# Rows of tokens from the vector engine's 32x32 transposes and a detour through DRAM, in place of TensorE's transposes

## The chip, the cores and the metric

The kernel runs on one core of one Trainium2 chip. The metric is the device time of one execution in microseconds (us). Three runs of the kernel before took 2768.79, 2769.45 and 2770.16 us; the median, 2769.45, is the time before.

## The reference

One step of a one-layer hybrid encoder for 256 prompt tokens and 64 sample tokens (320 together, the T of the code), model width 4096. What matters here is the outer frame; the mixer itself (attention heads and state-space heads behind the projection `w_in`) is untouched.

```python
def trunk_layer(x, p, ...):                       # x: (1, 256, 4096) or (1, 64, 4096)
    h = rmsnorm(x, norm_pre)
    m, k_new, v_new, conv_new, ssd_new = hybrid_mixer(h, ..., w_in, ..., w_out)
    x = x + rmsnorm(m, norm_post)
    e = p @ w_ple_proj                            # p has 256 features
    gate = jax.nn.sigmoid(x @ w_ple_gate)
    x = x + rmsnorm(gate * e, ple_norm)
    return x, ...                                 # y_prompt, y_sample: rows of tokens
```

`rmsnorm` divides a token's row by the root of its mean square and multiplies each feature by a weight. With r_m and r_g for the two factors of a token, the output is y = x + r_m * (m * norm_post) + r_g * (gate * e * ple_norm).

## The kernel before

**Weights.** All projections run with features on the partitions and the 320 tokens on the free axis. The weights come in blocks of 512 x 256 (512 KB, one DMA `raw` on SyncE's queue, line 155, four buffers). ScalarE rounds a block to `whi` (line 158), VectorE takes the rest `wlo` (line 159), three buffers each, and TensorE does 24 matmuls of 128 x 128 on 320 columns with the block (lines 163 to 165: whi*ahi, whi*alo, wlo*ahi). There are 720 blocks: 448 of `w_in`, 128 of `w_out`, then 128 of `w_ple_gate` and 16 half blocks of `w_ple_proj`. Eight blocks (kg 0 to 7) give one pair: two feature tiles of 128 rows, as two accumulators in PSUM. There are 16 pairs.

**Order.** `project` runs through the blocks; work behind a pair is a generator, and `tick` takes every pending generator one step further with each block. A scheduler turns the program into one fixed list of instructions for each engine, and each engine does its list in order, so an instruction that waits holds everything behind it on its engine. SyncE issues the DMAs in the order of its list too.

**From the output projection on.** `put_m` keeps the pairs of m, with `norm_post`, in eight group tiles. After r_m, `load_x2` forms x = xt + r_m * m for a group at a time, split into `ahi` and `alo`, while the first three gate pairs are projected together (`joint`, 8 x 3 blocks). This is the transition between the two phases. `put_pair` makes gate * e for a pair (`gate_out`, lines 335 to 346) and `two` with `ple_norm`. Between the gate pairs the half blocks of `w_ple_proj` make the next e (`embed`).

**Back to rows of tokens.** `to_token_rows` transposes each pair on TensorE (line 847; lines 854 and 855 for the sample's rows, once in two pairs) and ScalarE copies it out. `residual` does the same for x by products of `ahi` and `alo` with an identity (line 876; lines 882 and 884 for the sample): four units ahead of the end of the last gate pair, the other 16 behind it. After r_g, `finish` adds r_g * g to each unit on VectorE (line 920). SyncE stores eight column groups of 512: y_prompt by line 923, y_sample by line 926, whose pattern is `[2, 64, 256]`: two column halves, 64 tokens, 256 columns.

Of the kernel before, what the change touches and what calls it, by code (L numbers as in the profile page):

```python
# [41 lines left out]
def hymba_step(  # L42
# [17 lines left out]
    # what lives in one half of the kernel: the mixers, or the projections behind them  # L60
# [91 lines left out]
    def weights(src, kg, c0, nk=KG):  # L152
        """nk row tiles of NCOL columns, split exactly into two parts of 12 bits."""
# [13 lines left out]
    # Work behind a projection, as generators that pause between their stages; projections take  # L167
    # them one step further with each group of rows, so that the tensor engine finds their operands ready.
# [44 lines left out]
    def rsqrt_mean(out, total, n, shape):  # L213
        """out = (total / n + EPS) ** -0.5, with one step of Newton's method."""
# [8 lines left out]
    def factor_of(sqs, n):  # L223
        """The norm's factor of each token, on all partitions, from partial sums of squares."""
# [13 lines left out]
    class Squares:  # L238
        """Sum over `count` feature tiles of squares; the last one stays apart."""
# [3 lines left out]
        def add(self, make):  # L243
            """make(tile, soon) squares the next feature tile."""
# [16 lines left out]
    xt_dram = dram.tile([P, NK, T], F32, name="xt_dram")  # L261
    u_dram = dram.tile([P, 16, T], F32, name="u_dram")
    ssq = const1.tile([P, 3, NG], F32, name="ssq")
# [61 lines left out]
    def gate_in(g):  # L325
        """-g, bounded below as the exponential's argument is above."""
# [4 lines left out]
    def gate_out(es, vals, outs):  # L331
        """out = val / (1 + exp(-g)) for each e of gate_in(g); the quotient by one step of Newton's method."""
# [22 lines left out]
    def put_u(i, ap_mul):  # L355
        """Unit i (16 of each mixer) of the mixed output before its norm."""
# [10 lines left out]
    def to_rows(t, h, dst_p, dst_s, n):  # L367
        """A head's keys or values, back in rows of tokens."""
# [50 lines left out]
    def stick(h, i, q, k, vn, ck, cv, gss):  # L419
# [15 lines left out]
        # softplus(z), and log sigmoid(z) over z  # L435
# [33 lines left out]
    def steps():  # L469
        """dt of each token and head (tokens on partitions), dt * a, and decays."""  # L470
# [512 lines left out]
```

## Time and profile before

| what | us |
|---|---|
| median of three runs | 2769.45 |
| the profiled execution, its span (the only time of its own that its page gives) | 2768.3 |
| TensorE busy in it | 2741.7 (99%) |
| VectorE, ScalarE busy | 1450.8 (52%), 1110.9 (40%) |
| from the last gate matmul (2722.3) to the end | 46.0 |

The page's shares are of the span. "PEclk" in a row of windows is the granted clock of TensorE as a share of its full speed, 1.00 or 0.50 being its two levels, 2.4 and 1.2 GHz, and what lies between a mixture. In rows of instructions the arrow means "made from"; `L163` is line 163. The ends of matmuls are modelled; their distance in the chain of waits is the better price.

### The profile page before, as it was taken

How to read it: one execution, taken by the hardware profiler on the slowest of the kernel's cores; microseconds unless marked ns; L12 is line 12 of the kernel's file. 1: busy time of each engine (PE TensorE's matmuls, PEld its weight loads, DVE VectorE, ACT ScalarE, POOL GpSimd, SP SyncE). 2: the span in 40 equal slices, each digit the busy share in tenths (PEclk: the TensorE clock that was granted, in tenths of full speed). 3: DMA queues.
4: the chain of work that ended last, by engine and by line, in shares of the span. 5: the costliest groups of instructions: out<-in, count | busy, mean ns of one | idle time of the engine just before them, and what ended most of it. 6: DMA issues, size and time to landing. Idle time of an engine off the chain costs nothing.

```text
span 2768.3 us, 45230 instructions
## 1 busy us (share of the span) xinstructions
PE 2741.7 (99%) x18710; PEld 2713.2 (98%) x18710; DVE 1450.8 (52%) x2155; ACT 1110.9 (40%) x1551; POOL 241.5 (9%) x327
## 2 busy tenths in 40 slices
PE   9999999999999999999999999999999999999998
PEld 8999999999999999999999999999999989999997
DVE  4566666666666534435354453653333386454453
ACT  5443334433344333424333343543333354444441
POOL 0000010010000000000000000000101032121110
PEclk9999999999999999999999999999999999999997
DMA  7645454454454554555555455555444464444442
GB/s 236 194 120 145 132 149 138 127 164 127 143 148 134 149 153 143 151 149 146 152 143 157 140 150 161 168 162 159 148 150 152 137 191 147 150 144 151 149 142 84
DMA packets 419183, 414.13 MB, mean 150 GB/s; under 512 B 21792, under 2 KB 410784, under 8 KB 418976
## 3 DMA queue, kind: packets, MB, share of 16 engines
q1 hardware_dynamic: 418976, 411.24, 50.2%
q8 instruction: 146, 2.39, 0.3%
q14 instruction: 61, 0.50, 0.0%
HBM read 390.64 MB, written 20.55 MB: 149 GB/s over the span
## 4 chain that ended last, share of the span: by engine, by line
PE 96%; issue 1%; POOL 1%; DMA 1%; DVE 0%; ACT 0%; SPq 0%; DVEq 0%; POOLq 0%; ACTq 0%
PE acc L163 30%; PE acc L165 29%; PE acc L164 29%; POOL ug L817 1%; PE px L876 1%; DMA raw<-in_w_in_dram 1%; PE aux L665 1%; PE aux L372 0%; PE aux L492 0%; PE aux L557 0%; PE aux L847 0%; PE aux L453 0%; PE aux L666 0%; PE aux L426 0%; PE aux L651 0%
## 5 line engine op out<-in xcount | busy, mean ns | idle before, releaser
L163 PE MATMUL acc<-ahi,whi 128*128 128x320 f32 x5632 | 1757.6, 312 | 0.0
L165 PE MATMUL acc<-ahi,wlo 128*128 128x320 f32 x5632 | 1741.6, 309 | 3.6 <-DVE wlo L159 3.6
L164 PE MATMUL acc<-alo,whi 128*128 128x320 f32 x5632 | 1742.2, 309 | 1.3 <-DVE alo L819 1.2
L159 DVE TENSOR_TENSOR wlo<-raw,whi 128x1024 fp32r<-128x1024 f32 (+1 forms) x720 | 888.9, 1236 | 1119.6 <-ACT whi L158 1109.6
L158 ACT CAST whi<-raw 128x1024 fp32r<-128x1024 f32 (+1 forms) x720 | 747.1, 1038 | 1369.3 <-PE acc L164 1328.0
L165 PEld LDWEIGHTS acc<-ahi,wlo 128*128 128x128 f32 x5632 | 1058.5, 188 | 5.4 <-DVE wlo L159 5.4
L164 PEld LDWEIGHTS acc<-alo,whi 128*128 128x128 f32 x5632 | 1059.7, 188 | 2.5 <-DVE alo L819 2.3
L163 PEld LDWEIGHTS acc<-ahi,whi 128*128 128x128 f32 x5632 | 1059.3, 188 | 2.5
L252 POOL TENSOR_TENSOR stat<-stat,w 128x320 f32<-128x320 f32 x88 | 117.5, 1335 | 596.8 <-ACT w L779 404.6
L236 POOL TENSOR_TENSOR w<-ug 128x320 f32<-128x320 f32 x26 | 31.1, 1197 | 947.2 <-DVE ug L457 687.5
L335 ACT ACTIVATE w<-w 128x320 f32<-128x320 f32 (+1 forms) x96 | 45.1, 470 | 101.6 <-DVE w L328 101.5
L342 DVE SCALAR_TENSOR_TENSOR w<-w 128x320 f32<-128x320 f32 (+1 forms) x96 | 51.3, 541 | 16.3 <-ACT w L340 16.3
L236 POOL TENSOR_TENSOR w<-w 128x320 f32<-128x320 f32 x29 | 31.1, 1071 | 296.4 <-DVE w L346 296.4
L550 DVE SCALAR_TENSOR_TENSOR w<-w,vec 128x323 f32<-128x323 f32 x96 | 53.1, 553 | 2.1
L338 ACT ACTIVATE w<-w,tiny 128x320 f32<-128x320 f32 (+1 forms) x96 | 52.3, 560 | 2.9
L340 ACT ACTIVATE w<-w,shift 128x320 f32<-128x320 f32 (+1 forms) x96 | 52.2, 559 | 1.4
L344 DVE SCALAR_TENSOR_TENSOR w<-w 128x320 f32<-128x320 f32 (+1 forms) x96 | 49.6, 529 | 1.2
L545 POOL COPY ctail<-w 128x3 f32<-128x3 f32 x32 | 6.1, 190 | 328.3 <-DVE w L543 328.3
L328 DVE TENSOR_SCALAR w<-acc 128x320 f32<-128x320 f32 x32 | 15.6, 488 | 24.8 <-PE acc L165 24.7
L817 POOL TENSOR_TENSOR ug<-ug,two 128x320 f32<-128x320 f32 x16 | 23.7, 1486 | 43.2 <-DVE ug L816 43.2
L818 ACT CAST ahi<-ug 128x320 fp32r<-128x320 f32 x32 | 14.4, 461 | 25.8 <-POOL ug L817 22.4
L636 DVE TENSOR_SCALAR b<-le,dtah 128x256 fp32r<-128x256 f32 (+2 forms) x96 | 24.7, 292 | 0.0
(270 smaller groups left out, 1476.7 us busy)
## 6 DMA issues: line engine op xcount, KB each, us to landing
raw<-in_w_in_dram SPq DMA_DIRECT2D x448, 512.0 KB, 3.7
raw<-in_w_out_dram SPq DMA_DIRECT2D x128, 512.0 KB, 3.6
raw<-in_w_ple_gate_dram SPq DMA_DIRECT2D x128, 512.0 KB, 3.6
xt_dram<-ug SPq DMA_DIRECT2D x8, 640.0 KB, 6.2
two<-xt_dram SPq DMA_DIRECT2D x16, 320.0 KB, 3.3
b<-in_x_prompt_dram SPq DMA_DIRECT2D x16, 256.0 KB, 4.7
out_dram<-nat SPq DMA_DIRECT2D x32, 128.0 KB, 1.8
raw<-in_w_ple_proj_dram SPq DMA_DIRECT2D x16, 256.0 KB, 2.7
```

Source lines behind the costliest of these rows:

```text
L158: S.copy(hi, raw)
L159: V.tensor_sub(lo, raw, hi.bitcast(F32))
L163: PE.matmul(out, whi, xhi, start=start, stop=False)
L164: PE.matmul(out, whi, xlo, start=False, stop=False)
L165: PE.matmul(out, wlo, xhi, start=False, stop=stop)
L236: G.tensor_mul(sq, t, t)
L252: G.tensor_add(self.sum, self.sum, sq)
L338: S.activation(r, e, AF.Ln, scale=2.0 ** -62, bias=tiny)
L340: S.activation(r, r, AF.Exp, scale=-1.0, bias=shift)
L342: V.scalar_tensor_tensor(out=e, in0=e, scalar=1.0, in1=r, op0=ALU.add, op1=ALU.mult)
L550: V.scalar_tensor_tensor(out=c, in0=ext[:, j:j + XE], scalar=vec3[:, j * 32 + ct:j * 32 + ct + 1], in1=c, op0=ALU.mult, op1=ALU.add)
L817: (G if j % 2 else V).tensor_add(m, m, xt[:, j % 2, :])
```

## The change

The mixer output m (after `norm_post`) and the gated embedding (after `ple_norm`) go back to rows of tokens without TensorE. `to_token_rows` now takes a pair, does two VectorE transposes, each of 128 x 320 in blocks of 32 x 32, and writes the result with eight DMAs on SyncE into a DRAM tensor of rows (`m_rows` or `t_rows`). One DMA is 32 x 10 x 32: 320 runs of 32 floats, 128 bytes each. It is done for the 16 pairs of m during the output projection and for the 16 gate pairs.

`make_base`, started behind the joint gate pairs, takes r_m to the partitions (`r_tok`: three products with a diagonal and three sums), loads the rows of x from the inputs into the eight group tiles, loads the rows of m, and adds r_tok * m on VectorE: 24 additions. `fetch_rows`, during the last gate pair, loads the rows of the gated embedding for seven of the eight groups into buffers of `ahi` and `alo`; the eighth group's come after that pair. Behind r_g there are 24 additions r_g * g and the stores, y_sample's now on ScalarE's queue. `residual`, `some_residuals` and `finish` are gone.

```diff
-    ident_r = const.tile([P, P], F32R, name="ident_r")
-    V.tensor_copy(ident_r, ident)
+    stack = const.tile([P, 64], F32, name="stack")
+    V.tensor_add(stack, ident[:, 0:64], ident[:, 64:128])
...
+    def to_token_rows(fp, src, dst):
+        t = two()
+        for k in range(2):
+            V.transpose(out=t[:, k, :], in_=src[:, k, :])
+        yield 2
+        for k in range(2):
+            for a in range(4):
+                f0 = fp * NCOL + k * P + 32 * a
+                SY.dma_start(dst[:, f0:f0 + 32].rearrange("(b i) j -> i b j", i=32),
+                             t[32 * a:32 * a + 32, k, :].rearrange("p (b j) -> p b j", j=32))
...
         for i, acc in enumerate(accs):
             put_m(fp * 2 + i, acc)
+        start(to_token_rows(fp, m_groups[-1][:, fp % 2 * 2:fp % 2 * 2 + 2, :], m_rows), 1)
...
-        pairs.append(t)
-        start(to_token_rows(fp, t), 5)
...
+        start(to_token_rows(fp, t, t_rows), 1)
...
+    def load_rows(t, prompt, sample, g, ws=(0, 1, 2), to=None):
+        cs = slice(g * 512, (g + 1) * 512)
+        for w in ws:
+            c0, n = w * 512 if to is None else to, 256 if w == 2 else 512
+            SY.dma_start(t[:, c0:c0 + n], sample[:, cs].rearrange("t (u c) -> u t c", u=2) if w == 2
+                         else prompt[w * P:(w + 1) * P, cs])
+    def add_scaled(out, w, rows, factors):
+        c0, n = w * 512, 256 if w == 2 else 512
+        V.scalar_tensor_tensor(out=out[:, c0:c0 + n], in0=rows[:, 0:n], scalar=factors[:, w:w + 1],
+                               in1=out[:, c0:c0 + n], op0=ALU.mult, op1=ALU.add)
+    def make_base():
+        r_tok = const.tile([P, 3], F32, name="r_tok")
+        for w in range(3):
+            n = 64 if w == 2 else P
+            d = small((P, n))
+            V.tensor_mul(d, r_m[:, w * P:w * P + n], stack if w == 2 else ident)
+            V.reduce_sum(r_tok[:, w:w + 1], d, axis=mybir.AxisListType.X)
+        yield 1
+        for g in range(NG):
+            t = rows_tile(group())
+            load_rows(t, x_prompt[0], x_sample[0], g)
+            for w in range(3):
+                mt = rows_tile(two())
+                load_rows(mt, m_rows[0:TP], m_rows[TP:T], g, (w,), 0)
+                yield 2
+                add_scaled(t, w, mt, r_tok)
+            base.append(t)
+    def fetch_rows():
+        yield 4
+        for g in range(NG - 1):
+            late_rows.append(rows_tile(actp.tile([P, KG, T], F32, tag=("ahi", "alo")[g % 2], name="rows")))
+            load_rows(late_rows[-1], t_rows[0:TP], t_rows[TP:T], g)
+            if g % 2:
+                yield 1
...
     start(put_joint())
+    start(make_base(), 2)
     for fp in range(3, 16):
         if fp == 15:
-            start(some_residuals(4), 1)
+            start(fetch_rows(), 1)
...
+    drain()
+    late_rows.append(rows_tile(actp.tile([P, KG, T], F32, tag="alo", name="rows")))
+    load_rows(late_rows[-1], t_rows[0:TP], t_rows[TP:T], NG - 1)
...
+    for g, (t, y) in enumerate(zip(late_rows, base)):
+        cs = slice(g * 512, (g + 1) * 512)
+        for w in range(3):
+            add_scaled(y, w, t[:, w * 512:], r_g)
+        SY.dma_start(y_prompt[0][:, cs].rearrange("(w p) c -> p w c", p=P),
+                     y[:, 0:1024].rearrange("p (w c) -> p w c", w=2))
+        S.dma_start(y_sample[0][:, cs].rearrange("t (u c) -> u t c", u=2), y[:, 1024:1280])
```

Two places show how instructions move. The first is SyncE's list during the last two gate pairs. Of the kernel before, from the last half block of `w_ple_proj` on (a `raw` is one block of weights; `out_dram<-ug` with 128 partitions is y_prompt, with 2x64x256 y_sample):

```order
L155 DMA raw<-in_w_ple_gate_dram 128x4x256 x8
L155 DMA raw<-in_w_ple_proj_dram 128x2x256
L155 DMA raw<-in_w_ple_gate_dram 128x4x256 x40
L923 DMA out_dram<-ug 128x2x512 x2
L926 DMA out_dram<-ug 2x64x256 x2
```

The same stretch of the changed kernel, from the stores of pair 13's rows to the last block of weights (`rows<-t_rows` 128x512 is a load of prompt rows, 128x1x256 of sample rows; 32x10x32 is a store of eight DMAs for a pair):

```order
L788 DMA t_rows<-two 32x10x32 x8
L156 DMA raw<-in_w_ple_gate_dram 128x4x256 x7
L862 DMA rows<-t_rows 128x512 x2
L862 DMA rows<-t_rows 128x1x256
L862 DMA rows<-t_rows 128x512 x2
L788 DMA t_rows<-two 32x10x32 x8
L862 DMA rows<-t_rows 128x1x256
L862 DMA rows<-t_rows 128x512 x2
L862 DMA rows<-t_rows 128x1x256
L862 DMA rows<-t_rows 128x512 x2
L862 DMA rows<-t_rows 128x1x256
L156 DMA raw<-in_w_ple_gate_dram 128x4x256
```

Before, the last 40 blocks stand in one run with nothing between them; after, the last block of the last pair stands behind the loads of four groups' rows and the stores of pair 14's.

The second place is VectorE's list behind the joint gate pairs, where the first gated pairs are made. Before (`wlo` is half of a block of weights, lines 342 to 346 are the quotient of a gated pair):

```order
L159 TENSOR_TENSOR wlo<-raw,whi 128x512
L342 SCALAR_TENSOR_TENSOR w<-w 128x320 x2
L344 SCALAR_TENSOR_TENSOR w<-w 128x320 x2
L346 SCALAR_TENSOR_TENSOR w<-w,e 128x320 x2
L159 TENSOR_TENSOR wlo<-raw,whi 128x1024
L342 SCALAR_TENSOR_TENSOR w<-w 128x320 x2
L344 SCALAR_TENSOR_TENSOR w<-w 128x320 x2
L346 SCALAR_TENSOR_TENSOR w<-w,e 128x320 x2
L159 TENSOR_TENSOR wlo<-raw,whi 128x1024
L159 TENSOR_TENSOR wlo<-raw,whi 128x512
```

And after, from the last of that piece's whole blocks on (`r_tok` is the factor of the tokens, `ug<-two,r_tok,ug` an addition to the base):

```order
L160 TENSOR_TENSOR wlo<-raw,whi 128x1024
L878 TENSOR_TENSOR w<-stat,ident 128x128 x2
L879 TENSOR_REDUCE r_tok<-w 128x1 x2
L878 TENSOR_TENSOR w<-stat,stack 128x64
L783 STREAM_TRANSPOSE two<-two 128x320
L879 TENSOR_REDUCE r_tok<-w 128x1
L783 STREAM_TRANSPOSE two<-two 128x320
L160 TENSOR_TENSOR wlo<-raw,whi 128x512
L345 SCALAR_TENSOR_TENSOR w<-w 128x320
L347 SCALAR_TENSOR_TENSOR w<-w 128x320
L160 TENSOR_TENSOR wlo<-raw,whi 128x1024
```

Between two `wlo` that stood next to each other before, there are now eight VectorE instructions, and between later ones additions to the base and more transposes.

## Rows read from the trace of the kernel before

**Rows 1.** The page: span, busy time of engines, landing of the weights' DMAs

```profile
span 2768.3 us, 45230 instructions
...
PE 2741.7 (99%) x18710; PEld 2713.2 (98%) x18710; DVE 1450.8 (52%) x2155; ACT 1110.9 (40%) x1551; POOL 241.5 (9%) x327
...
raw<-in_w_ple_gate_dram SPq DMA_DIRECT2D x128, 512.0 KB, 3.6
```

**Rows 2.** Timeline of ScalarE, 2199.5 to 2211: start, duration, instruction, [idle before, releaser]

```profile
2199.82 1.05 ACT L158 CAST whi<-raw 128x1024 fp32r<-128x1024 f32 x1 [2.47 <-PE acc L164]
...
2210.38 1.05 ACT L158 CAST whi<-raw 128x1024 fp32r<-128x1024 f32 x1 [2.47 <-PE acc L164]
```

**Rows 3.** Timeline of SyncE's DMA issues, 2196 to 2203

```profile
2198.63 0.37 SPq L155 DMA_DIRECT2D raw<-in_w_out_dram  x1
```

**Rows 4.** Timeline of VectorE, 2199 to 2205

```profile
2200.90 1.23 DVE L159 TENSOR_TENSOR wlo<-raw,whi 128x1024 fp32r<-128x1024 f32 x1 [2.29 <-ACT whi L158]
```

**Rows 5.** TensorE's groups, 2340 to 2722.1: count | busy, mean ns | idle before

```profile
L847 PE MATMUL aux<-ident,two 128*128 128x128 f32 x60 | 9.0, 272 | 0.0
L854 PE MATMUL aux<-ident,two 128*128 128x128 f32 x14 | 3.4, 273 | 0.0
L855 PE MATMUL aux<-ident,two 128*64 128x128 f32 x14 | 3.4, 273 | 0.0
L876 PE MATMUL px<-ident_r,alo 128*128 128x128 f32 x12 | 2.8, 275 | 0.0
```

**Rows 6.** Chain of waits, 2354 to 2356: start, length, what

```profile
2354.47 0.44 PE aux L847 x4
```

**Rows 7.** Chain of waits, 2690 to 2770

```profile
2698.10 0.84 PE px L876 x8
...
2722.43 0.50 DVE w L328
```

**Rows 8.** Windows: stretch, us, PE PEld DVE ACT POOL busy (x), PEclk, DMA share, GB/s

```profile
2722.30:2733.00 10.70, 10.47 (x82) 10.17 (x81) 6.95 (x15) 5.72 (x14) 0.87 (x1) 0.77 0.01 2
2733.00:2756.20 23.20, 22.65 (x113) 21.89 (x112) 12.04 (x21) 0.00 (x0) 0.00 (x0) 0.52 0.54 187
2756.20:2766.80 10.60, 0.00 (x0) 0.00 (x0) 0.36 (x1) 0.00 (x0) 0.00 (x0) 0.62 0.23 84
```

**Rows 9.** DMA, 2762 to 2766: packets, MB, share of 16 engines' time

```profile
q1 hardware_dynamic: 190, 0.19, 13.5%
```

**Rows 10.** Timeline of VectorE, 2730.5 to 2730.9

```profile
2730.54 0.16 DVE L221 SCALAR_TENSOR_TENSOR r_g<-stat,r_g 128x3 f32<-128x3 f32 x1
```

**Rows 11.** Timeline of SyncE's DMA issues, 134.5 to 135.7

```profile
135.11 0.47 SPq L375 DMA_DIRECT2D out_dram<-nat  x1
```

**Rows 12.** Chain of waits, 2284.9 to 2288

```profile
2284.93 0.27 PE acc L163
...
2287.60 0.27 PE acc L164
```

**Rows 13.** Windows of the transition and of the first gated pairs

```profile
2280.00:2285.00 5.00, 3.06 (x19) 2.79 (x18) 5.00 (x10) 3.40 (x6) 1.15 (x2) 0.94 0.28 95
...
2330.00:2340.00 10.00, 10.00 (x70) 10.00 (x70) 9.40 (x13) 7.68 (x15) 7.26 (x6) 1.00 0.36 106
```

**Rows 14.** Timeline of VectorE, 2340 to 2342

```profile
2340.21 1.21 DVE L159 TENSOR_TENSOR wlo<-raw,whi 128x1024 fp32r<-128x1024 f32 x1
```

**Rows 15.** Timeline of TensorE, 2341.5 to 2342.6

```profile
2342.28 0.31 PE L165 MATMUL acc<-ahi,wlo 128*128 128x320 f32 x1
```

**Rows 16.** VectorE's groups, whole span

```profile
L328 DVE TENSOR_SCALAR w<-w 128x320 f32<-128x320 f32 (+1 forms) x64 | 20.7, 323 | 1.4
L920 DVE SCALAR_TENSOR_TENSOR ug<-ug,r_g,y 128x512 f32<-128x512 f32 x4 | 2.7, 748 | 0.0
```

**Rows 17.** DMA, 121.5 to 122.0, the column of `w_in` for dt

```profile
DMA packets 246, 0.03 MB, mean 60 GB/s; under 512 B 246, under 2 KB 246, under 8 KB 246
...
q1 hardware_dynamic: 246, 0.03, 38.6%
```

More of the change, by code (lines that the diff above doesn't have):

```diff
@@ L262, in hymba_step @@
     u_dram = dram.tile([P, 16, T], F32, name="u_dram")
+    m_rows = dram.tile([T, D], F32, name="m_rows")
+    t_rows = dram.tile([T, D], F32, name="t_rows")
     ssq = const1.tile([P, 3, NG], F32, name="ssq")
@@ L821, in load_x2 @@
         return x_parts[g]
-    pairs, g_rows = [], []
     gsq = Squares(NK)
@@ L834, in put_pair @@
             S.activation(t[:, i, :], s, AF.Copy, scale=n_ple[:, fp * 2 + i:fp * 2 + i + 1])
-        pairs.append(t)
-        start(to_token_rows(fp, t), 5)
-    def to_token_rows(fp, t):
-        if fp % 2 == 0:
-            g_rows.append(group().rearrange("p k t -> p (k t)"))
-        rows, half = g_rows[fp // 2], fp % 2
-        pt = aux()
-        for i in range(2):
-            for w in range(2):
-                PE.transpose(pt[:, w * NCOL + i * P:w * NCOL + (i + 1) * P], t[:, i, w * P:(w + 1) * P], ident)
-        S.copy(rows[:, 0:1024].rearrange("p (w a c) -> p w a c", w=2, a=2)[:, :, half, :],
-               pt.rearrange("p (w c) -> p w c", w=2))
-        if half:
-            pt = aux()
-            for i in range(2):
-                PE.transpose(pt[:, i * P:(i + 1) * P], t[:, i, TP - 64:T], ident)
-                PE.transpose(pt[0:64, i * P:(i + 1) * P], pairs[fp - 1][:, i, TP:T], ident)
-            S.copy(rows[:, 1024:1280], pt[:, 0:NCOL])
-        yield 1
@@ L859, in hymba_step @@
-    joint = project([(w_ple_gate[0], 0, "acc"), (w_ple_gate[0], NCOL, "acc"), (w_ple_gate[0], 2 * NCOL, "aux")], load_x2)
-    units = []
-    for gp in range(NG // 2):
-        for g in (2 * gp, 2 * gp + 1):
-            units += [(0, [g]), (1, [g])]
-        units.append((2, [2 * gp, 2 * gp + 1]))
-    def residual(n, tag="aux"):
-        w, groups = units[n]
-        px = ps.tile([P, 512], F32, tag=tag, name="px", bufs=4)
-        for k, g in enumerate(groups):
-            if w < 2:
-                for j in range(KG):
-                    for i, t in enumerate(x_parts[g]):
-                        PE.matmul(px[:, j * P:(j + 1) * P], t[:, j, w * P:(w + 1) * P], ident_r,
-                                  start=i == 0, stop=i == 1)
-                continue
-            for j in range(2):
-                cs = slice((2 * k + j) * P, (2 * k + j + 1) * P)
-                for i, t in enumerate(x_parts[g]):
-                    PE.matmul(px[:, cs], t[:, 2 + j, TP - 64:T], ident_r, start=i == 0, stop=i == 1)
-                for i, t in enumerate(x_parts[g]):
-                    PE.matmul(px[0:64, cs], t[:, j, TP:T].bitcast(F32), ident, is_transpose=True,
-                              start=i == 0, stop=i == 1)
-        return px
@@ L888, in hymba_step @@
-    pxs = []
-    def some_residuals(count):
-        for _ in range(count):
-            y = pool["wk"].tile([P, 2, T], F32, tag="e", name="y", bufs=5).rearrange("p a t -> p (a t)")[:, 0:512]
-            S.copy(y, residual(len(pxs)))
-            pxs.append(y)
-            yield 2
+        start(to_token_rows(fp, t, t_rows), 1)
+    joint = project([(w_ple_gate[0], 0, "acc"), (w_ple_gate[0], NCOL, "acc"), (w_ple_gate[0], 2 * NCOL, "aux")], load_x2)
+    base, late_rows = [], []
+    def load_rows(t, prompt, sample, g, ws=(0, 1, 2), to=None):
[4 more added lines that the diff above has]
+                         else prompt[w * P:(w + 1) * P, cs])
@@ L913, in hymba_step @@
             embed()
-    def finish(n, px):
-        w, groups = units[n]
-        for k, g in enumerate(groups):
-            cols = 512 if w < 2 else NCOL
-            y = g_rows[g][:, w * 512:w * 512 + cols]
-            V.scalar_tensor_tensor(out=y, in0=y, scalar=r_g[:, w:w + 1], in1=px[:, k * cols:(k + 1) * cols],
-                                   op0=ALU.mult, op1=ALU.add)
-            if w == 1:
-                SY.dma_start(y_prompt[0][:, g * 512:(g + 1) * 512].rearrange("(w p) c -> p w c", p=P),
-                             g_rows[g][:, 0:1024].rearrange("p (w c) -> p w c", w=2))
-            elif w == 2:
-                SY.dma_start(y_sample[0][:, g * 512:(g + 1) * 512].rearrange("t (a c) -> a t c", a=2), y)
-    banks = 0
-    for _ in range(4):
-        banks += 1
-        pxs.append(residual(len(pxs), ("acc", "aux")[banks % 2]))
+    drain()
+    late_rows.append(rows_tile(actp.tile([P, KG, T], F32, tag="alo", name="rows")))
+    load_rows(late_rows[-1], t_rows[0:TP], t_rows[TP:T], NG - 1)
     r_g = const.tile([P, 3], F32, name="r_g")
```

8 lines of the change are left out of this document (2 added, 6 removed).

## Prediction

> **What bounds the kernel now.** I read the page first: TensorE is busy for 2741.7 of 2768.3 us [rows 1], so the end is set by its work and by the gaps that others leave it. Then how much slack its suppliers have in the steady part. ScalarE's casts of whole blocks start at 2199.82 and, three blocks on, at 2210.38 [rows 2]: 10.56 / 3 = 3.52 us for a block, 24 matmuls of 0.147. Each cast was released by TensorE, which freed one of three buffers: two more blocks, 7.04 us, run before its own is needed, and cast and rest take 1.05 + 1.23 [rows 2, 4], so 4.7 us are spare there. The DMA issued at 2198.63 [rows 3] fills the fourth cast, at 2210.38: 11.75 us later, where landing takes 3.6 [rows 1], so 8.1 spare. A weight load may come 8.1 + 4.7 = 12.9 us late in the steady part before TensorE stalls. Last the two places where there is no such cover: the transition with the first gated pairs, where VectorE is busy for 5.00 of 5 and 9.40 of 10 us [rows 13], and the tail behind the last gate matmul at 2722.3, 46.0 us [rows 7, 8], where TensorE's residuals fill 23 us and then two DMA engines alone work: 13.5% of sixteen is 2.2 engines [rows 9].
>
> **The change part by part**, against the profiled execution's 2768.3, which lies 1.15 below the median.
>
> *TensorE's work.* What goes before the last gate matmul stands beside nothing else, TensorE being full: 60 matmuls of line 847 and 14 + 14 of lines 854 and 855 [rows 5] at 0.44 / 4 = 0.11 [rows 6] make 9.7; residuals of three units (12 of `alo`, as many of `ahi`) at 0.84 / 8 [rows 5, 7] make 2.5. Sum **-12.2**. Both ends of this term are near, since nothing of it overlaps.
>
> *The last block of weights.* Here SyncE's list holds, ahead of the last `raw`, loads of four groups' rows and pair 14's eight stores. The price of a group: 190 packets in 4 us on 13.5% of sixteen engines [rows 9] is 45 ns for 1 KB. Before, y_sample's stores run on two engines; a load of sample rows has the same two halves, 64 tokens and 256 columns, so I take the same two engines for it: 64 packets each, 2.9 us. A load of 128 prompt rows is 128 packets of 2 KB over sixteen engines, at twice the price 0.7 us. So a group takes 2.9 + 1.4 = 4.3 us on the two slow engines, and a block of weights, 512 packets over sixteen, 1.4.
> The rule that bears on it is in the Trainium skill, "DMA: Bandwidth & Descriptors", section "Why a DMA increments its semaphore by 16 and not by 1": a transfer uses the largest number of engines up to 16 that divides the slowest dimension of both patterns. By it these loads, with an outer dimension of 2 in DRAM, use 2 engines; the trace shows it for stores of that pattern only.
> Count from the end of the last pair's first block: loads issue at +1.4; the first two groups' prompt rows and one sample load take 4 x 0.7 + 2.9, to +7.1. Pair 14's rows come out of its quotient and the transposes; eight issues of 0.47 [rows 11] follow from +4.5, done at some +9.5. Behind them one sample load and two whole groups, 2.9 + 8.6, to +21.0; the block 1.4, to +22.4; landing +0.9, cast and rest 2.3: +25.6. TensorE wants it after six more blocks, at +21.1. A stall of 4.5 us. After the transition's gap TensorE ran at half clock, 0.27 a matmul from 2284.93 to 2287.87 [rows 12], some 1.5 us lost; I add the same. **+6.0**, bounds 0 (loads on sixteen engines) and +10 (stores' completion 3 to 4 us later than taken).
>
> *The tail.* In the 33.8 us from 2733.0 to 2766.8 [rows 8] the two slow engines carry 8 groups of stores, 4.2 us each. Now they get the last group's rows as well, **+4.2**; stores start after r_g, at 2730.7 [rows 10], as before, y_sample's on ScalarE's own queue, so not behind pair 15's stores on SyncE. If they do start behind these, 2 us more. VectorE's 24 additions, 16 x 0.75 and 8 x 0.48 by line 920's row for 512 columns [rows 16], take 16 us and are hidden; so is TensorE, which has left. Bounds +1 and +6.
>
> *VectorE behind the joint gate pairs.* The rest of a block computed at 2340.21 to 2341.42 is used at 2342.28 [rows 14, 15]: 0.9 us spare, less still at the next. Ahead of the next half block there now stand three products, three sums and two transposes, and before the following blocks an addition and two transposes more. Nearest row for a transpose: 323 ns from SBUF on 128 x 320 [rows 16] at the low end, 748 ns x 320 / 512 = 0.47 at the other; I take 0.45, and 0.25 for a small product or sum. 6 x 0.25 + 0.9 + 0.7 + 0.9 = 4.0, less 0.9: **+3**, bounds 0 (if VectorE's waits for ScalarE take it up) and +6 (a transpose at twice that).
>
> *The transition.* There VectorE is the bound [rows 13], and pair 15's m brings two transposes to its list: **+1**, bounds -4 and +4, since the order of 32 other instructions there changes too.
>
> *At nothing.* Stores of 128 bytes in the steady part: the only short packets in the trace are reads, 246 in 0.5 us on 38.6% of sixteen engines [rows 17], 12.6 ns each. A pair writes 8 x 320 = 2560, 160 on each engine: 2.0 us, and SyncE's eight issues 3.8 us. Together 5.8, under the 12.9 of slack. The writes eat it up from (12.9 - 2.2) / 160 = 67 ns a packet, five times the reads' price. I take the reads' price, the only row.
> The Trainium skill, same page, section "Specifications", says that below 512 bytes an engine reads, changes and writes back. No row here shows a short write; by that rule, at twice the reads' price, a pair takes 4 us and still nothing is late.
> Loads of the rows of x, six sample loads at 2.9 among six blocks of the joint pairs: up to 13 us late against 12.9, so 0, at worst +3. VectorE's steady pairs: 0.9 us of transposes in 28 us, 52% busy [rows 1], hidden.
>
> Sum -12.2 + 6.0 + 4.2 + 3 + 1 = +2.0: 2770.3, and with the 1.15 to the median **2771**.
>
> **Rivals.**
> *A: the sample loads use all sixteen engines.* They are loads, and no row shows a load of this pattern. Then a group takes 0.4 + 1.4 us, the last block lands in time, and the tail gains only +2: -12.2 + 2 + 3 + 1 = -6.2: 2763. Against it: stores of the same pattern do run on two [rows 9]. Chance 0.27.
> *B: VectorE waits for rows of m.* Its additions to the base stand in its list ahead of rests of weights, and the loads of m's rows stand on SyncE behind `raw`s that wait for buffers and behind stores that wait for a pair's transposes. An addition whose rows land 2 us or more after VectorE comes to it delays the rest behind it; from the 4.7 us less 1 to 2.7 of other work, 2 to 3.7 us of wait are free. If seven pairs with such additions lose 2 us each: 2771 + 14 = 2785; if only four, 2779. For it: the order puts several such loads just three blocks before their use. Against it: a load of 0.7 us of engine time lands within 3.6 where the queue is free. Chance 0.23, time 2783 (six pairs).
> *C: short writes cost far more than short reads.* Each 10 ns over 67 costs 1.6 us in each of some 28 pairs: at 85 ns already 2771 + 80, and at 70 ns 2784. For it: no row prices a short write. Against it: a write would have to cost five times a read of its length. Chance 0.06, 2800 and more.
>
> **How the numbers follow.** My forecast, 2771, has 0.44. Its own range: the distances of the bounds of its last four terms from the values taken, squared and added, give 8.9 down (6.0, 3.2, 3, 5) and 6.1 up (4, 1.8, 3, 3): 2762 to 2777. About what a measurement of this kernel tells from no change is 0.2%, 5.5 us: 2764 to 2775. Of my forecast 0.06 lies below that, 0.28 within, 0.10 above; of A 0.16, 0.10 and 0.01; of B 0.04 within and 0.19 above; C's 0.06 above. Faster 0.22, same 0.42, slower 0.36. The range, 2761 to 2788, leaves out the lower half of A's faster part, C, and the end of B, some 0.2.
>
> **What would show it.** Lines 847, 854, 855 and 876 gone from TensorE, and the time of the last gate matmul 2722.3 - 12.2 plus what stalls add. On TensorE a gap of about 4.5 us before the last block of the last pair, released by the rest of that block, with half clock behind it; the last load landing some 20 us after the row loads were issued. Gaps in TensorE before the first gated pairs, put down to VectorE. In the tail a row of two engines' share (13%) and a length of about 50 us from the last gate matmul. Packets of 128 bytes at about 13 ns in windows of a pair's stores. I am wrong if sample loads spread over sixteen engines (faster), if TensorE waits for VectorE in the later pairs, or if short writes take over 67 ns.

## The result, and the profile after

The changed kernel takes 2791.5 us (median of 4 runs, 2790.85 to 2793.87) against 2769.8 beside it: a ratio of 1.0078, interval 1.0064 to 1.0092. It is slower by 21.7 us, where 2771 was forecast, and lies above the range. Its profiled execution spans 2789.7 us, 21.4 more than that of before.

The page of the changed kernel, in the form of [rows 1]: span and busy times, then two groups of TensorE, whose last column is the idle time before them and what ended it. The line by itself is the group of before that waited most for weights.

```profile
span 2789.7 us, 45100 instructions
...
PE 2707.7 (97%) x18422; PEld 2675.2 (96%) x18422; DVE 1496.6 (54%) x2249; ACT 1098.4 (39%) x1523; POOL 234.7 (8%) x327
...
L164 PE MATMUL acc<-ahi,whi 128*128 128x320 f32 x5632 | 1758.5, 312 | 10.7 <-ACT whi L159 10.7
...
L166 PE MATMUL acc<-ahi,wlo 128*128 128x320 f32 x5632 | 1743.6, 310 | 12.2 <-DVE wlo L160 12.1
```

```profile
L165 PE MATMUL acc<-ahi,wlo 128*128 128x320 f32 x5632 | 1741.6, 309 | 3.6 <-DVE wlo L159 3.6
```

TensorE has 288 matmuls less and is 34 us less busy, part of it from residuals in the tail. But it now waits some 23 us for weights (3.6 before), rounded (ScalarE) or their rest (VectorE). Where, is read from the distance of the first matmuls of consecutive blocks of weights: what it has above 3.52 us (1.76 for a half block) is lost, or is other work of TensorE's. The table gives the sum of these excesses for each stretch, in us. Blocks are counted from 0 through all 720; the first three pairs of the output projection end at 471.

| stretch of blocks | before | after | difference | forecast |
|---|---|---|---|---|
| 470 to 499: first row stores of m | 1.2 | 4.6 | +3.4 | 0 |
| 576 to 603: transition, joint gate pairs | 10.3 | 8.9 | -1.4 | +1 |
| 604 to 608: just behind the joint gate pairs | 0.0 | 7.7 | +7.7 | 0 |
| 609 to 639: first gated pairs | 3.1 | 11.5 | +8.4 | } +3, and -12.2 |
| 640 to the end of the last gate matmul | 9.5 | 8.2 | -1.3 | } +6 |
| behind it: the tail | 46.0 | 50.7 | +4.7 | +4.2 |

The 3.1 and 9.5 of before are its transposes and residuals, 12.6 us, all gone in the changed kernel: from block 640 to the last but one it loses nothing (0.0 us). So the two places marked } are +11.5 and +8.2 of new stalls. The sum is -12.6 + 3.4 - 1.4 + 7.7 + 11.5 + 8.2 + 4.7 = 21.5. (The row of the transition tells nothing: in kernels that are alike there it came out between 7.0 and 11.5. The blocks before 470, where no experiment edits anything, also scatter: 180.6 us in the changed kernel, 181.3 in that of before, up to 184.1 in the others.)

Windows of the changed kernel, columns as in [rows 8]:

```profile
2326.00:2340.00 14.00, 10.74 (x66) 9.32 (x64) 7.25 (x14) 6.76 (x13) 0.55 (x1) 1.00 0.59 179
2340.00:2390.00 50.00, 40.96 (x242) 38.64 (x243) 36.07 (x52) 24.03 (x42) 15.05 (x15) 0.93 0.59 156
2390.00:2715.00 325.00, 325.00 (x2218) 325.00 (x2217) 182.91 (x226) 141.61 (x199) 51.87 (x44) 1.00 0.61 177
2715.00:2739.00 24.00, 18.57 (x110) 17.87 (x108) 3.61 (x4) 3.09 (x4) 0.00 (x0) 0.86 0.54 161
```

TensorE is idle for 3.3 us of 14, 9.0 of 50 and 5.4 of 24, and for none of the 325 between, where each pair's transposes and eight stores run all the time. In the first gated pairs VectorE is busy for 36 of 50 us (30 in the 50 us of before from 2330): it has more to do. From 2337 to 2363 it is nearly full, 23.3 of 26 us; behind that it waits.

What ended last stands in the chain of waits, 2322 to 2392 (start, length, what):

```profile
2315.69 8.79 DMA raw<-in_w_ple_gate_dram
2324.52 10.51 DMA raw<-in_w_ple_proj_dram
2335.13 0.62 ACT whi L159
...
2363.40 6.57 DMA two<-m_rows
2370.05 0.34 issue
2370.39 1.23 DVE wlo L160
```

A block that landed in 3.6 us [rows 1] lands in 8.8, a half block in 10.5. From 2335 to 2358 the chain then runs through the lists of ScalarE and VectorE alone. And a load of m's rows, issued at 2363.40, keeps VectorE, and the rest of a block behind its addition, until 2370. Why these loads are late says a stretch of the DMA just after that half block was issued, and SyncE's waits from 2320 to 2390 (engine, line, what it waited for: us in all, times, longest):

```profile
q1 hardware_dynamic: 33, 0.04, 13.4%
```

```profile
SPq L156 <- DVE wlo L160: 11.6, 5, 4.8
SPq L788 <- DVE two L783: 8.4, 2, 6.4
...
SPq L862 <- DVE two L783: 3.5, 1, 3.5
```

From 2326.9 to 2327.7 only 13.4% of the sixteen engines work, 2.1 of them, as at y_sample's stores [rows 9]: sample rows are still coming in on two engines while a half block of weights waits behind them. The updates of the blocks' semaphores show the same: of the block issued at 2315.69, fourteen of sixteen shares have landed by 2321.3, the last two at 2324.2 and 2324.5; of a block of before issued at 2316.22, all sixteen land between 2319.2 and 2319.9. SyncE itself is held too: the half block's issue takes it 2.98 us here, 0.39 in e1 below:

```profile
2324.52 2.98 SPq L156 DMA_DIRECT2D raw<-in_w_ple_proj_dram  x1
```

```profile
2314.04 0.39 SPq L156 DMA_DIRECT2D raw<-in_w_ple_proj_dram  x1
```

And SyncE stands 8.4 us before row stores whose transposes VectorE hasn't made, and 3.5 before a load of m's rows for which no buffer is free; all weights of its list stand behind. But not every such wait costs something. 2.0 of the 8.4, the 3.5 and eight issues lie between 2346.67 and 2357.41, when SyncE issues no weights for 10.7 us. The other 6.4, up to 2381.59, hold weights back, but behind block 618 TensorE loses nothing. (Its waits for `wlo`, for a free buffer of weights, are its usual pace.)

### The profile page after: what moved, and what is told of

Read it like the earlier page. It is cut to its first block, busy times and chain, and to the rows that moved or that the text cites. A ratio compares the mean times of both kernels' runs of the same rounds, so it can differ in the third digit from the quotient of the medians.

```text
span 2789.7 us, 45100 instructions
## 1 busy us (share of the span) xinstructions
PE 2707.7 (97%) x18422; PEld 2675.2 (96%) x18422; DVE 1496.6 (54%) x2249; ACT 1098.4 (39%) x1523; POOL 234.7 (8%) x327
## 4 chain that ended last, share of the span: by engine, by line
PE 92%; DMA 3%; DVE 2%; ACT 1%; issue 0%; SPq 0%; POOL 0%; DVEq 0%; ACTq 0%; POOLq 0%
PE acc L164 29%; PE acc L166 29%; PE acc L165 29%; DMA raw<-in_w_ple_gate_dram 1%; DVE wlo L160 1%; DMA raw<-in_w_in_dram 1%; PE aux L668 1%; DMA raw<-in_w_ple_proj_dram 0%; PE aux L375 0%; DMA out_dram<-ug 0%; DMA rows<-t_rows 0%; PE aux L495 0%; PE aux L560 0%; DVE ug L867 0%; DVE ug L832 0%
## 5 line engine op out<-in xcount | busy, mean ns | idle before, releaser
L164 PE MATMUL acc<-ahi,whi 128*128 128x320 f32 x5632 | 1758.5, 312 | 10.7 <-ACT whi L159 10.7
L166 PE MATMUL acc<-ahi,wlo 128*128 128x320 f32 x5632 | 1743.6, 310 | 12.2 <-DVE wlo L160 12.1
L164 PEld LDWEIGHTS acc<-ahi,whi 128*128 128x128 f32 x5632 | 1061.2, 188 | 14.7 <-ACT whi L159 12.2
L237 POOL TENSOR_TENSOR w<-w 128x320 f32<-128x320 f32 x29 | 23.6, 814 | 303.9 <-DVE w L349 303.9
L867 DVE SCALAR_TENSOR_TENSOR ug<-two,r_tok,ug 128x512 f32<-128x512 f32 (+1 forms) x24 | 18.9, 788 | 20.0 <-DMA two<-m_rows 20.0
L833 POOL TENSOR_TENSOR ug<-ug,two 128x320 f32<-128x320 f32 x16 | 21.7, 1361 | 52.1 <-DVE ug L832 20.1
## 6 DMA issues: line engine op xcount, KB each, us to landing
xt_dram<-ug SPq DMA_DIRECT2D x8, 640.0 KB, 12.1
```

The source lines that it names most:

```text
L164: PE.matmul(out, whi, xhi, start=start, stop=False)
L166: PE.matmul(out, wlo, xhi, start=False, stop=stop)
L237: G.tensor_mul(sq, t, t)
```

## The experiments

The theories: **L**, loads of sample rows on two engines hold the weights; **S**, the row stores in SyncE's list hold what is behind them, by their issues or their waits; **P**, the short packets hold the engines; **V** with rival B, VectorE's added work and its additions that wait for rows of m. With each edit the scheduler also lays out all engines' lists anew; where that matters, it is said. Times are medians beside a kernel before of 2770.9 to 2771.5 us in the same job (2769.8 beside the changed kernel), ratios against it. Losses by stretch are from the profiled executions, worked out as in the table above.

| run | us | ratio, interval | 470-499 | 604-608 | 609-639 | 640-end | tail |
|---|---|---|---|---|---|---|---|
| changed kernel | 2791.5 | 1.0078, 1.0064-1.0092 | 4.6 | 7.7 | 11.5 | 8.2 | 50.7 |
| e1_spread | 2773.0 | 1.0006, 0.9996-1.0015 | 3.4 | 0.0 | 10.6 | 1.2 | 47.9 |
| e2_one_store | 2762.3 | 0.9968, 0.9955-0.9981 | 1.2 | 0.0 | 1.9 | 0.2 | 48.2 |
| e3_no_m | 2787.6 | 1.0057, 1.0042-1.0072 | 4.6 | 6.7 | 7.8 | 8.1 | 50.5 |
| e4_stagger | 2791.6 | 1.0071, 1.0056-1.0086 | 1.2 | 6.1 | 14.1 | 8.9 | 50.7 |
| e5_spread_all | 2755.1 | 0.9940, 0.9925-0.9955 | 1.2 | 0.1 | 10.5 | 1.3 | 32.6 |
| e6_act_stores | 2795.2 | 1.0086, 1.0071-1.0101 | 3.6 | 0.0 | 21.4 | 8.2 | 48.7 |
| e7_before_spread | 2755.9 | 0.9949, 0.9933-0.9966 | 1.2 | 0.0 | 3.1 | 9.5 | 29.3 |
| e8_long_runs | 2763.2 | 0.9974, 0.9963-0.9984 | 1.2 | 0.0 | 2.0 | 0.2 | 48.0 |
| e9_base_later | 2750.6 | 0.9927, 0.9912-0.9941 | 1.2 | 0.1 | 5.4 | 0.9 | 32.9 |
| e10_rows_later | 2747.5 | 0.9918, 0.9901-0.9934 | 1.2 | 0.1 | 0.7 | 0.6 | 32.6 |
| e11_waits_only | 2785.8 | 1.0048, 1.0031-1.0065 | 3.4 | 6.2 | 3.2 | 9.1 | 50.1 |

In e3, e4 and e11 the stall of blocks 604 to 608 ends one block later: in each of them 1.8 us of the column 609-639 belong to it (0.2 in the changed kernel).

**e1_spread: sample loads on sixteen engines.**

```diff
-            SY.dma_start(t[:, c0:c0 + n], sample[:, cs].rearrange("t (u c) -> u t c", u=2) if w == 2
-                         else prompt[w * P:(w + 1) * P, cs])
+            if w == 2:
+                for u in range(2):
+                    SY.dma_start(t[u * 64:u * 64 + 64, c0:c0 + n], sample[:, g * 512 + u * 256:g * 512 + u * 256 + 256])
+            else:
+                SY.dma_start(t[:, c0:c0 + n], prompt[w * P:(w + 1) * P, cs])
```

> Each load of sample rows (of x, m and the gated embedding) becomes two loads of 64 rows of 1 KB, u = 0 and u = 1, so that none has the outer dimension of 2; all else as in the changed kernel (2791.5 us, profiled 2789.7). Theory L (loads on two engines hold the weights behind them): the stalls of 7.6 us in the blocks just before the first gated pairs shrink to 2 or less, the 5.6 us before the last block to under 2, the tail by 3 to 5: 2778. Theory V (VectorE's added work and its waits are the cause there): the stalls before the first gated pairs stay, only the last block's and the tail's part go: 2783 to 2785. If loads ran on sixteen engines before too: no change, or slower by the 24 more issues.

The stall before the first gated pairs is gone (7.7 to 0.0), that before the last block all but gone (8.2 to 1.2), the tail 2.8 shorter: 18.5 us, more than L expected. Two engines were the cause at all three places, and V's reading of the first falls. The 10.6 us among the first gated pairs stay, at three places: 2.1 at blocks 612 and 613, where rests of weights stand behind VectorE's quotients, transposes and an addition; 3.1 at 614 and 615, where weights and rows of m land late; and 5.2 at 617, where casts stand behind other work in ScalarE's list (shown at e9).

**e2_one_store: one DMA of long runs a pair.**

```diff
-        for k in range(2):
-            for a in range(4):
-                f0 = fp * NCOL + k * P + 32 * a
-                SY.dma_start(dst[:, f0:f0 + 32].rearrange("(b i) j -> i b j", i=32),
-                             t[32 * a:32 * a + 32, k, :].rearrange("p (b j) -> p b j", j=32))
+        SY.dma_start(flat(dst, 20 * fp, 20, 640), t.rearrange("p k t -> p (k t)"))
...
```

Not shown: the loads, which read these runs back as they lie, and e1's edit.

> As e1_spread, and a pair's 320 KB go to DRAM in one DMA of 128 x 640 instead of eight of 320 runs of 128 bytes; the loads read back as many bytes in as many loads. What this leaves out is the order of the rows: the elements land in other places, so the output is permuted. Theory S (eight issues a pair on SyncE, and their waits, hold weights and loads of m): beyond e1_spread, the 4.6 us at the burst of the first three pairs' stores in the output projection go, and at least half of the 11.3 us among the first gated pairs: 2768 to 2772. Theory V: the burst's goes, the 11.3 stay: 2774 or as much below e1_spread as 3 to 4 us.

Beyond e1, 10.7 us go: burst and first gated pairs. VectorE's transposes, factors and additions are all still there, so V is worth at most the 1.9 that remain, 1.6 of them at one block. Issue, wait and packet length are not told apart yet.

**e3_no_m: no loads of m's rows, no additions to the base.**

```diff
-            for w in range(3):
-                mt = rows_tile(two())
-                load_rows(mt, m_rows[0:TP], m_rows[TP:T], g, (w,), 0)
-                yield 2
-                add_scaled(t, w, mt, r_tok)
+            yield 6
             base.append(t)
```

> The changed kernel without the 24 loads of m's rows and without the 24 additions to the base; r_m * m is missing from the output, everything else stays (transposes, stores, loads of x and of the gated embedding). Theory V with rival B (additions that wait for rows of m): the stalls of 11.3 us among the first gated pairs go to under 3, those of 7.6 us before them stay: 2780. Theory S: only the part with an addition waiting for its load goes (4.5 us), the one behind eight stores stays: 2785.

Of the 11.5 us among the first gated pairs 3.7 go, 7.8 stay; counted from block 610 on, 11.3 become 6.1. The loads, the additions and their waits go together here, so rival B's mechanism is real, but at most a third to a half of the stall, and in the first pairs alone.

**e4_stagger: the first three pairs' stores apart.**

```diff
-        start(to_token_rows(fp, m_groups[-1][:, fp % 2 * 2:fp % 2 * 2 + 2, :], m_rows), 1)
+        start(to_token_rows(fp, m_groups[-1][:, fp % 2 * 2:fp % 2 * 2 + 2, :], m_rows), 1 + 3 * fp if fp < 3 else 1)
```

> The changed kernel with the row stores of the first three pairs of m started 1, 4 and 7 blocks behind their joint projection instead of all at 1, so that three blocks of weights stand between each eight stores. If the burst of 24 issues on SyncE is what delayed one block there (4.6 us at two blocks, 1.1 of it at another block before the change too): that stall goes, -3.4 us, 2788; if the short packets themselves hold the weights' transfers: the stall spreads and the time stays at 2791.

The stall of the burst goes as expected (4.6 to 1.2; 1.1 of that are TensorE's own transposes of the input p). In the changed kernel SyncE's burst, the landing of the four blocks of weights issued right behind it (from 1860.29 to 1861.88), and ScalarE's next casts read:

```profile
1846.51 13.67 SPq L788 DMA_DIRECT2D m_rows<-two  x24
```

```profile
raw<-in_w_out_dram SPq DMA_DIRECT2D x4, 512.0 KB, 4.9
```

```profile
1868.25 1.00 ACT L771 CAST pl<-aux 128x320 fp32r<-128x320 f32 x2 [10.08 <-PE aux L770]
1869.15 2.94 ACT L159 CAST whi<-raw 128x1024 fp32r<-128x1024 f32 x3
```

For 13.7 us no weights are issued, 0.57 us an issue, with 12.9 of slack. But it is not a late landing that TensorE waits for: these land some 5 us behind their issues, the first two by 1866, and the first cast comes at 1869.15. ScalarE stood 10.08 us before two casts of p, which its list has ahead and which wait for TensorE's transposes of p. The changed kernel, e1, e3 and e11 all have this wait of 10.08 us and lose 3.4 to 4.7 us; in before, e2, e4, e5, e8, e9 and e10 the casts of p stand behind casts of weights, and 1.2 is lost. So the burst brought the stall, but by way of the order that the scheduler gave ScalarE's list. 1.2 of the 4.6 is half clock, which e1 has not (PEclk 0.83 from 1870 to 1880, in e1 1.00). The time does not move: 3.4 us fewer there, but 1.7 more before block 470, where nothing was edited, 1.1 more from block 610 to 639 (the other 1.5 of that column's rise is the stall that ends one block later) and 0.7 at the last block. Why these rose is open.

**e5_spread_all: e1, e4 and y_sample's stores on sixteen engines.** **e7_before_spread: the kernel before with those stores alone.**

```diff
-        S.dma_start(y_sample[0][:, cs].rearrange("t (u c) -> u t c", u=2), y[:, 1024:1280])
+        for u in range(2):
+            S.dma_start(y_sample[0][:, g * 512 + u * 256:g * 512 + u * 256 + 256], y[u * 64:u * 64 + 64, 1024:1280])
```

(e5's edit; e7 has the same two stores on SyncE's queue, where before had its one.)

> e1_spread (2773.0 us) with the first three pairs' stores of m staggered as in e4_stagger, and y_sample's stores in two of 64 rows each as its loads are there. If two engines set the end of the tail (47.9 us behind the last block in e1_spread): the tail goes to VectorE's 24 additions and one last landing, some 32 us, -15; the burst -3: 2755. If the tail is set by the chain from r_g through VectorE instead: -3 only, 2770. The 10.6 us among the first gated pairs stay in both.

> The kernel before with each store of y_sample as two of 64 rows. If two engines set the end of its 46 us tail: the end moves to the last residual on TensorE (33.4 us behind the last gate matmul) and a landing, -9 or -10: 2760. If not: no change, 2770. It tells how much of a gain of e5_spread_all would have been to be had without the change.

The tail falls from 47.9 to 32.6, and in the kernel before from 46.0 to 29.3: there more than expected. Three windows of e5's tail:

```profile
2721.90:2732.00 10.10, 2.55 (x16) 2.37 (x16) 6.91 (x17) 4.62 (x11) 1.15 (x1) 0.61 0.21 35
2732.00:2744.00 12.00, 0.00 (x0) 0.00 (x0) 11.72 (x21) 0.00 (x0) 0.00 (x0) 0.50 0.70 221
2744.00:2754.50 10.50, 0.00 (x0) 0.00 (x0) 0.48 (x1) 0.00 (x0) 0.00 (x0) 0.50 0.86 304
```

VectorE's additions fill the second window, then all the engines of the DMA carry the last stores at 304 GB/s, where the tail of before ended at 84 [rows 8]. Both kernels gain alike from it, so none of this gain belongs to the change: e5 and e7 are level. That e7 gained more than expected lies in TensorE's residuals, which were taken at the half clock of [rows 8]; the last window of e7 has them at 0.91 (why, is open; one of its four runs, with a mean granted clock of 0.994 against 0.997 and 0.998 of the others, took 2761.6 us):

```profile
2742.00:2754.30 12.30, 6.68 (x64) 6.41 (x62) 5.40 (x9) 0.00 (x0) 0.00 (x0) 0.91 0.70 250
```

**e6_act_stores: e1 with the row stores on ScalarE's queue.**

```diff
-                SY.dma_start(dst[:, f0:f0 + 32].rearrange("(b i) j -> i b j", i=32),
+                S.dma_start(dst[:, f0:f0 + 32].rearrange("(b i) j -> i b j", i=32),
```

> e1_spread (2773.0 us) with the eight stores of each pair issued from ScalarE's queue instead of SyncE's; same packets, same bytes. Theory S (issues and waits in SyncE's list hold weights and loads of m behind them): of the 10.6 us among the first gated pairs at least 6 go, and the burst of 24 in the output projection too: 2764. Theory P (the 128-byte packets themselves hold the weights' packets on the engines): both stay, 2773. A cost of its own: each issue takes ScalarE half a microsecond, 4 us a pair, beside casts; if these hold up casts, new stalls of TensorE released by ScalarE appear and the time is 2773 or more.

22 us slower than e1: 21.4 us among the first gated pairs (10.6 in e1) and 8.2 from there on (1.2). ScalarE's waits from 2320 to 2520:

```profile
ACT whi L159 <- PE acc L165: 39.6, 24, 4.2
ACT whi L159 <- DMA t_rows<-two: 31.7, 6, 8.6
```

The first row is the usual pace; the second is 31.7 us in which casts stood behind row stores in ScalarE's list, until earlier ones had landed. The wait in a list came along to ScalarE's list. It does not decide between S and P.

**e8_long_runs: eight DMAs a pair, but runs of 1280 bytes.**

```diff
+        rows = dst[20 * fp:20 * fp + 20, :].rearrange("t c -> (t c)")
         for k in range(2):
             for a in range(4):
-                f0 = fp * NCOL + k * P + 32 * a
-                SY.dma_start(dst[:, f0:f0 + 32].rearrange("(b i) j -> i b j", i=32),
-                             t[32 * a:32 * a + 32, k, :].rearrange("p (b j) -> p b j", j=32))
+                e0 = (4 * k + a) * 32 * T
+                SY.dma_start(rows[e0:e0 + 32 * T].rearrange("(p n) -> p n", n=T), t[32 * a:32 * a + 32, k, :])
...
```

Not shown: the loads, which read these runs back as they lie, and e1's edit.

> e1_spread (2773.0 us) with the same eight DMAs a pair on SyncE, the same bytes from the same partitions, but each partition's 320 floats go out as one run of 1280 bytes, and the loads read them back in as many loads. What this leaves out is the order of the rows: the output is permuted. Theory S (eight issues and their waits in SyncE's list): the 10.6 us among the first gated pairs and the 3.4 at the burst stay, 2771 to 2774. Theory P (short packets hold the engines, and so the weights): both go as in e2_one_store, 2762.

By its time P would have won. But it is not the clean test that it was meant to be: the scheduler gave these stores other places. SyncE's list at the burst:

```profile
1847.63 0.37 SPq L156 DMA_DIRECT2D raw<-in_w_out_dram  x1
1848.77 1.72 SPq L793 DMA_DIRECT2D m_rows<-two  x4
1851.15 0.39 SPq L156 DMA_DIRECT2D raw<-in_w_out_dram  x1
1851.64 9.28 SPq L793 DMA_DIRECT2D m_rows<-two  x20
```

A block of weights stands among the stores here, and blocks stand further ahead among the first gated pairs as well. Issues are shorter too, 0.46 us against 0.57. So it leaves P and S open.

**e9_base_later: e5 with the base made behind the first gated pairs.**

```diff
-    start(make_base(), 2)
+    start(make_base(), 26)
```

> e5_spread_all (2755.1 us) with make_base started 26 blocks behind the joint gate pairs instead of 2, so that r_tok, the loads of m's rows and the additions come behind the first gated pairs; their stores stay. Rival B alone there (additions waiting for rows of m, 4 to 5 us of the 10.6, by the two waits of VectorE seen) goes, and with r_tok's 3 us of VectorE the 1.8 at the second of these pairs: 2749. If the stores on SyncE alone make these stalls: 2755.

10.5 to 5.4, 4.5 us in time: additions, their loads and r_tok out of the way. Nothing is lost before block 617 now; the 5.4 are all at 617 and 618. SyncE still waits 8.5 us for transposes there, but that is not what holds these blocks. Their weights, how they land, and what ScalarE does before it casts them:

```profile
2354.80 1.50 SPq L156 DMA_DIRECT2D raw<-in_w_ple_gate_dram  x3
```

```profile
raw<-in_w_ple_gate_dram SPq DMA_DIRECT2D x3, 512.0 KB, 5.0
```

```profile
2364.30 0.56 ACT L849 ACTIVATE two<-w,vec 128x320 f32<-128x320 f32 x1 [1.84 <-DVE w L349]
2364.77 0.73 ACT L811 COPY e<-acc 128x320 f32<-128x320 f32 x2
2365.39 2.95 ACT L159 CAST whi<-raw 128x1024 fp32r<-128x1024 f32 x3
```

The second of the three, issued at 2355.30, has landed at 2360.3, and the first before it; the casts begin at 2365.39, because ScalarE's list has its whole share of a pair's quotient ahead of them. Neither packets nor SyncE's wait hold them.

**e10_rows_later: e9 with the stores two blocks later behind their transposes.**

```diff
         for k in range(2):
             V.transpose(out=t[:, k, :], in_=src[:, k, :])
-        yield 2
+        yield 4
```

> e9_base_later with the eight stores of each pair two blocks later behind their transposes (in both phases), so that SyncE does not come to a store before its transposes are done. Theory S: what is left among the first gated pairs (some 5 us) goes to 1 or 2: 4 us below e9_base_later, 2745. If the time of the issues alone holds the weights, not the waits: 1 us or nothing below it.

5.4 to 0.7, 3.1 us in time (2750.6 to 2747.5; the intervals of the two overlap, the profile's stretch is the better evidence). Packets and number of issues are as before. Two things went. SyncE's wait, from 2320 to 2390, in place of the 8.5 of e9:

```profile
SPq L788 <- DVE two L783: 0.4, 1, 0.4
```

And the order of ScalarE's list: two of the three casts now come ahead of the end of that share:

```profile
2362.89 1.98 ACT L159 CAST whi<-raw 128x1024 fp32r<-128x1024 f32 x2
2364.87 0.56 ACT L849 ACTIVATE two<-w,vec 128x320 f32<-128x320 f32 x1
```

By what ended last in e9, it is the second that counts; the place of the stores in the program decides both. P falls: the weights had landed. Of S, the wait falls for blocks 617 and 618, and stays for 614 and 615 of the changed kernel and e1, where casts begin when late weights land. e10 is also the fastest version tried, 2747.5 us against 2755.9 of e7: with its stalls mended and the stores of y_sample alike in both, the change is worth some 8 us (the two were timed in different jobs, and their intervals against before just touch).

**e11_waits_only: the changed kernel with the edits of e9 and e10 alone.**

> The changed kernel (2791.5 us) with the two edits of e9_base_later and e10_rows_later alone: make_base 26 blocks behind the joint gate pairs, and the eight stores of a pair two blocks later behind their transposes; the loads of sample rows stay as they are, on two engines. If the two causes add up: the 11.5 us among the first gated pairs go to 1 or 2 and the 7.6 before them, the last block's and the tail's stay: 2781. If the first gated pairs' stalls were only the echo of the late sample loads before them: 2788 or more.

11.5 to 3.2 without touching the sample loads; 6.2 and 9.1 at the sample loads' two places stay. With block 609 counted to the first of these, the sample loads cost 7.9 there in both kernels, and the first gated pairs 11.3 and 1.4. So the causes are separate and add up. The time, 2785.8, gains only 5.7, 5 us less than hoped: 3.5 lie in the blocks before 470, where nothing was edited, and 2.4 in the transition (11.3), both within the scatter there, 0.9 at the last block.

## Why the prediction was wrong, point by point

The forecast failed in two sentences of "At nothing", with a sum that otherwise held to some 2 us a term. The first booked loads of sample rows at nothing that took the whole slack, the second priced the row stores without the waits and the new orders that they bring.

- *TensorE's work*, -12.2: the 12.6 us are gone, and between 2390 and 2715 nothing takes their place. Right.
- *The last block of weights*, +6.0: 8.2 in the trace. The mechanism as forecast, behind sample loads on two engines: issued at 2720.82, the block's cast starts 10.97 us later; fourteen of its sixteen shares have landed by 2727.2, the last two at 2731.7 and 2731.8. e1 takes 7.0 of it away. The stall is 5.6 against 4.5, the rest half clock, as at [rows 12]. (No row shows the 0.9 of landing in that count.) The chain of waits from 2715 to the end:

```profile
2720.82 10.97 DMA raw<-in_w_ple_gate_dram
2731.89 1.05 ACT whi L159
2732.99 0.64 PE acc L164
2733.62 0.27 PE acc L165
...
2747.44 0.17 DVE r_g L222
2747.64 5.26 DVE ug L867 x9
2752.92 10.32 DMA out_dram<-ug
2763.26 9.54 DMA rows<-t_rows
2772.82 0.48 DVE ug L867
```

- *The tail*, +4.2: +4.7, in part by luck. Two engines, as forecast, but e1, which spreads the loads, takes only 2.8 of it away. The chain has a step that the sum lacked: the last group's rows are loaded behind y_prompt's first stores on SyncE and land at 2772.8, after VectorE's other additions.
- *"Loads of the rows of x, six sample loads at 2.9 among six blocks of the joint pairs: up to 13 us late against 12.9, so 0, at worst +3."* This failed: 7.7. The step weighed the two engines' time against the full slack of the steady part, and had the two equal: a margin of zero cannot be booked as nothing. The late weights also met the quotients of the three joint pairs, which stand between the rests in VectorE's list (the next block's cast came at 2337.8 and its rest, behind a pair's quotient, ended at 2341.4). Rival A's condition was false, and its price for these loads, 8 us between its time and the forecast, far too low: e1 gives 18.5.
- *"Stores of 128 bytes ... under the 12.9 of slack."* The price was right: 2678 short writes in 4 us of the burst on 50.8% of sixteen engines are 12.1 ns each. From 1852 to 1856, in the changed kernel:

```profile
DMA packets 2678, 0.33 MB, mean 82 GB/s; under 512 B 2678, under 2 KB 2678, under 8 KB 2678
...
q1 hardware_dynamic: 2678, 0.33, 50.8%
```

  By that row the engines are half idle in the burst, and rival C is out. The Trainium skill says ("DMA: Bandwidth & Descriptors", "Specifications") that below 512 bytes an engine reads, changes and writes back; if that makes a packet dearer than a read of its length, this row does not show it. What failed is the count of the lists: the step set the engines' time and SyncE's issues against the slack of the steady part, and priced no wait in any list. For a steady pair, 8 issues in 3.9 to 5.7 us, the 12.9 hold, and from block 640 to the last but one nothing is lost. Among the first gated pairs SyncE issues no weights from 2346.67 to 2357.41: 2.0 us for transposes, 3.9 of issues, 3.5 for a buffer. Weights and a load of m's rows are late behind that, 5.5 of the 11.5 us (blocks 614 and 615). The other part is the order of ScalarE's list, which the prediction did not look at: 2.7 at blocks 617 and 618, and at the burst casts of p ahead of weights, +3.4 with the half clock behind it. Together with the loads of m, the eight stores of a pair are worth 8.7 us among the first gated pairs (e1 to e2).
- *VectorE behind the joint gate pairs*, +3: its own work is worth at most 1.9 (e2). A transpose takes 0.49 to 0.51 us, near the 0.45 taken; the six small products and sums some 2.7 in all, not the 1.5 taken. The groups of the changed kernel:

```profile
L783 DVE STREAM_TRANSPOSE two<-ug 128x320 f32<-128x320 f32 x32 | 16.0, 505 | 7.1 <-ACT ug L795 7.1
L783 DVE STREAM_TRANSPOSE two<-two 128x320 f32<-128x320 f32 x32 | 14.6, 486 | 1.2 <-ACT two L849 1.2
L867 DVE SCALAR_TENSOR_TENSOR ug<-two,r_tok,ug 128x512 f32<-128x512 f32 (+1 forms) x24 | 18.9, 788 | 20.0 <-DMA two<-m_rows 20.0
```

- *Rival B*, 2783 at 0.23: the nearest to the time, for at most half of the reason. Its additions wait 20.0 us in all, but TensorE loses only 3.7 to 5.2 of that (e3), in the first gated pairs; seven pairs with 2 us each never came, since from 2390 on nothing stalls. It needed the stores to be late: the load at 2363.40 stood behind eight of them. (That load is one of sample rows, but two engines explain little of it: spread in e1, it still keeps VectorE 3.9 us, 5.1 here.)
- The Trainium skill's rule that the prediction cites for the last block ("DMA: Bandwidth & Descriptors", "Why a DMA increments its semaphore by 16 and not by 1") agrees with the trace for loads too: 13.4% in the stretch shown, and e1.

## What to carry to other kernels

A transfer on few engines is not slow by itself alone: every later transfer of the queue, split over all engines, lands when its share on the slow ones does, so a weight load behind small loads takes their time (8.8 us here in place of 3.6). In a queue that issues in order, price for each inserted DMA the issue, the wait for its producer and the wait for its buffer, and set their sum against the slack at the tightest place, not at the steady one. A cost that equals the slack is a stall, not a zero. And before a queue is blamed, see whether the data had landed: twice here they had, some 5 us before the cast, and what held it was an instruction that the scheduler had put ahead of it in another engine's list.

## What the runs showed of the hardware that was not expected

- Writing 320 runs of 128 bytes takes the engines no longer per run (12.1 ns) than reading such runs does (12.6, [rows 17]). The issue is somewhat longer: 0.57 us a DMA in a row of 24 and 0.48 in the quickest row of eight, against 0.46 with 32 runs of 1280 bytes (20 in 9.28 us).
- A store on ScalarE's queue held ScalarE's casts, 31.7 us in 200 (e6).
- Behind sample loads on two engines a block's shares land in two groups, fourteen and then two, some 3 us apart (4.5 at the last block), and SyncE's issues take up to 3 us.
- One pattern of 128 KB stores set 15 to 17 us of the tail (47.9 to 32.6, and in the kernel before 46.0 to 29.3).
